# A hybrid decoder step on one core: a list scheduler that accounts for the SBUF port shared by VectorE and GpSimd

## The chip, the cores and the metric

The kernel runs on 1 core of one Trainium2 chip. The metric is device time in microseconds (us), from one launch to its end. Lower is better.

## The reference, cut to what matters

One inference step of a decoder trunk with two layers, on 528 prompt rows (16 learned meta rows and 512 tokens) and 8 sample rows, 536 in all, with 1024 columns each, in float32. Each layer is:

```
x = x + 0.5 * SwiGLU_1(RMSNorm(x))
x = x + W_o(sig(gA) * RWKV7(.) + sig(gB) * ShortConv(.))
x = x + 0.5 * SwiGLU_2(RMSNorm(x))
```

RWKV7 is, for each of 16 heads of 64, a recurrence over rows with a matrix state S:

```
Sa = S a_t
S = S * w_t + Sa b_t^T + v_t k_t^T
y_t = S r_t
```

The prompt starts from S = 0; the 8 sample rows take one step each from a given state. The outputs are y for prompt and sample and all new states.

## The kernel before, in words

**Stages.** A feed-forward stage (`ffn`), the mixer of layer 0 (`mixer`), two feed-forwards, the mixer of layer 1, and a last feed-forward with the final norm. Activations lie with features on 128 partitions and rows along the free dimension. Weights come in tiles of 128 x 1024 (`load_split`): a DMA to `raw`, ScalarE rounds to `hi`, VectorE subtracts (`lo = raw - hi`, two inputs in SBUF), and each product is three passes, hi*hi, hi*lo and lo*hi (`mm3`).

**The mixer.** Heads go in 8 pairs p. `stage_k(p)` projects k and r, computes decays and the Gram products of 11 chunks of 48 rows, and inverts the triangular matrix of each chunk. `stage_v(p)` projects v and prepares `P1`. `chain(p)` runs over the 11 chunks in series: products `cq` on TensorE with steps `rh`, `rd`, `ud`, `sx`, `sd` between them on VectorE and ScalarE; its last state goes out by DMA to `o_swkv`. `gnorm(p)` is the group norm (`wm`), `stage_m(p)` the merge. The loop issues chain(p-1), gnorm(p-1), stage_k(p+1), stage_v(p) in this order. Forty gated projections (`gated_parts`, drawn by `fill`) have low priority and fill in between. `sample` makes the step of the 8 sample rows: eight slices of the state through GpSimd and VectorE operations of 512 columns (names s, t, VB, sm), then DMAs through `yd` to `yb`, transposes and products `ws`. After it the merged rows `mh` go into the product with `w_o` (acc<-mh).

**The inverse** (in `stage_k`, lines 1025 to 1071). The Gram blocks `GT` go by DMA to DRAM (`td`) and back as `Ta`, so that each of 88 partitions holds one half-chunk with half of its columns. Then 46 GpSimd operations, 23 products `pr` and 23 sums into `Xinv`, one after another. The result goes by DMA to `xd` and back as the diagonal blocks of `Yd`. For two groups of chunks, 6 and 5 (`SPL`), the function `step` then issues three rounds on TensorE into PSUM tile `w`, each evicted by ScalarE: transposes of Yd into `x1` (name w1; in the profile MATMUL w<-cst,Yd, as it is a product with the identity), `off` times x1 into `x2` (w2), and x2 times Yd back into Yd (w3). The chain's product cq<-rd,Yd needs the result. Tile w shares a PSUM bank with `cq` and `wm` of the pairs of the same parity.

**What sets the order.** Nothing is issued in program order. Class `Sched` records every operation (all show as line 271, in `issue`, the line that emits them), with its dependencies and a price (`price`, lines 140 to 164), and `flush` (lines 284 to 336) simulates the five engines' queues: it takes the engine that can go on earliest, and on it, of the operations that are ready at that time, the one with the smallest sequence number less `boost`. This fixes each engine's instruction order. On the chip each engine then takes its instructions in that order and waits where an input is late. `offer` (lines 246 to 263) hands an operation to its queue once its buffers are free. All DMAs are on the queue of SyncE (SP). The prices that the change touches, in us for n columns:

```
VectorE       0.07 + n/960, two inputs in SBUF outside the feed-forward n/860; three inputs 0.13
GpSimd        0.2 + n*3e-3, in the feed-forward 0.1 + n*3.1e-3
```

`nc.ffn` is the flag that tells which; `ffn` sets and clears it.

Of the kernel before, what the change touches and what calls it, by code (L numbers as in the profile page):

```python
# [12 lines left out]
PSUM = bass.MemoryType.PSUM  # L13
DRAM = bass.MemoryType.DRAM
# [30 lines left out]
            vector=('bv', 'ka', 'kh', 'kql', 'kt', 'm', 'mb', 'rk', 'rnip', 'rt', 's1', 's3a', 'sl', 'u', 'yl', 'zg')),  # L45
       dict(boost={'k': 1500, 'v': -1000, 'c': 2000, 'g': 100, 'f': -3000, 'm': -50, 's': 1000, 'i': 1500, 'w': 50, 'e': -2000, 'h': -2000},
            ka=4, gated=[0, 3, 0, 0, 1, 0, 0, 1, 1, 0, 2, 2, 1, 0, 0, 1, 0, 0, 1, 4, 1, 0, 1, 0, 1, 1, 0, 1, 1, 1, 0, 0],
            same=0, inv=(),
            vector=('bv', 'kh', 'kql', 'kt', 'm', 'mb', 'rk', 'rt', 's3a', 'sl', 'u', 'yl', 'zg'))]
FIRST = -300  # L50
NORM = 1000
SETUP = -60
# [21 lines left out]

class Op:
    __slots__ = ("seq", "eng", "fn", "args", "kw", "cost", "lat", "npred", "succ", "ready", "prio", "tiles", "first",
                 "tab", "cols0", "cols")


class Slots:  # L80
# [17 lines left out]
class Sched:  # L98
# [13 lines left out]
    def __init__(self, tc):  # L112
        self.nc = tc.nc
        for e in ENGINES:
            setattr(self, e, Engine(self, e))
        self.ops, self.acc, self.free, self.slots, self.life = [], {}, {}, {}, {}
        self.same, self.ffn = 0, False
        self.tick, self.cols, self.fast = 0, 0.0, False
        self.table, self.end, self.gate, self.dma, self.boost, self.kept, self.coming = None, 0.0, 0.0, 0.0, 0, [], []

# [19 lines left out]
    def price(self, eng, fn, out, ins, kw):  # L140
        n = self.width(out)
        if fn == "dma_start":
            return 0.48, 4 * n * out.shape[0] / self.DMA_RATE
        if eng == "tensor":
            if fn == "transpose" or kw.get("is_transpose"):
                return n / 1200 + 2e-3, self.HOP
            return (max(n, 256) / 2400 + 12e-3 if ins[0].dtype == F32R else n / 600 + 6e-3), self.HOP
        if eng == "vector":
            if fn == "memset":
                return 8e-3 + n / 960, self.HOP  # L150
            if fn == "reciprocal":
                return 0.12 + n * 6.16e-3, self.HOP
            if fn == "tensor_reduce":
                n = self.width(ins[0])
            fixed = 0.13 if len(ins) > 2 else 0.07
            if not self.ffn and len(ins) > 1 and all(x.tensor.space != PSUM for x in ins):
                return fixed + n / 860, self.HOP
            return fixed + n / 960, self.HOP
        if eng == "scalar":
            psum = any(x.tensor.space == PSUM for x in ins + [out])  # L160
            return (0.05 if psum else 0.095) + (0.09 if "scale" in kw else 0) + n / 1200, self.HOP
        if self.ffn:
            return 0.1 + n * 3.1e-3, self.HOP
        return 0.2 + n * 3e-3, self.HOP

    def add(self, eng, fn, args, kw):
        o = Op()
        o.seq, o.eng, o.fn, o.args, o.kw = len(self.ops), eng, fn, args, kw
        out = kw["out"] if "out" in kw else args[0]
        ins = [x for x in list(args) + list(kw.values()) if hasattr(x, "tensor") and x is not out]  # L170
        o.cost, o.lat = self.price(eng, fn, out, ins, kw)
        o.tab = TABLES.get(kw.get("func")) if eng == "scalar" else None
        o.succ, o.ready, o.prio, o.first, o.tiles, o.npred = [], 0.0, o.seq - self.boost, [], [], 0
        if eng == "tensor":
            o.cols0 = (o.cost - 12e-3) * 2400
            o.cols = o.cols0 * ins[0].shape[0] / 128
        w = (kw["lhsT"] if "lhsT" in kw else args[1]) if eng == "tensor" else None
        preds, needs, opens = {}, {}, {}
        for ap, wr in [(x, False) for x in ins] + [(out, True)]:
            t = ap.tensor  # L180
            if not hasattr(t, "tag_meta"):
                continue
            n = t.name
            if n not in self.acc:
                self.acc[n] = [], []
                if t.space != DRAM:
                    key = str(t.cap_key)
                    if key not in self.slots:
                        self.slots[key] = Slots(key.rsplit('_', 2)[1], t.bufs or t.tag_meta.bufs, self.gate)
                    self.life[n] = Life(self.slots[key], o)  # L190
                    self.slots[key].line.append(n)
                    o.first.append(n)
            if n not in o.tiles:
                o.tiles.append(n)
                if n in self.life:
                    lf = self.life[n]
                    lf.left += 1
                    opens[id(lf.opener)] = lf.opener
                    if n in lf.slots.held:
                        lf.slots.held[n] = None  # L200
            b = self.box(ap)
            writes, reads = self.acc[n]
            for c, q in writes + reads if wr else writes:
                if c[0] < b[1] and b[0] < c[1] and c[2] < b[3] and b[2] < c[3]:
                    preds[id(q)] = q
                    if not wr:
                        needs[id(q)] = 3 if ap is w and w.dtype == F32 else 2
            if wr:
                for a in (writes, reads):
                    a[:] = [x for x in a if not (b[0] <= x[0][0] and x[0][1] <= b[1] and b[2] <= x[0][2] and x[0][3] <= b[3])]  # L210
                writes.append((b, o))
            else:
                reads.append((b, o))

        for q in {**opens, **preds}.values():
            if q is o:
                continue
            kind = needs.get(id(q), 1 if id(q) in preds else 0)
            if q.succ is None:
                self.follow(q, o, kind)  # L220
            else:
                q.succ.append((o, kind))
                o.npred += 1
        self.ops.append(o)
# [21 lines left out]
    def offer(self, o):  # L246
        for n in o.first:
            s = self.life[n].slots
            if s.line[0] != n or len(s.held) >= s.bufs and all(x is None for x in s.held.values()):
                s.waiting.append(o)  # L250
                return
        first, o.first = o.first, []
        for n in first:
            s = self.life[n].slots
            s.line.pop(0)
            o.ready = max(o.ready, s.gate)
            if len(s.held) >= s.bufs:
                old = min((x for x in s.held if s.held[x] is not None), key=s.held.get)
                o.ready = max(o.ready, s.held.pop(old))
            s.held[n] = None  # L260
        heapq.heappush(self.wait[o.eng], (o.ready, o.seq, o))
        for n in first:
            self.retry(self.life[n].slots)
# [22 lines left out]
    def flush(self):  # L286
# [8 lines left out]
        for _ in range(len(self.ops)):  # L295
            t, e = min((max(self.free.get(e, 0.0), 0.0 if avail[e] else self.wait[e][0][0]), e)
                       for e in ENGINES if avail[e] or self.wait[e])
            while self.wait[e] and self.wait[e][0][0] <= t:
                o = heapq.heappop(self.wait[e])[2]
                heapq.heappush(avail[e], (o.prio, o.seq, o))  # L300
            o = heapq.heappop(avail[e])[2]
# [12 lines left out]
                self.load_table(o.tab)  # L314
            if e == "tensor":
                c = self.clocked(o, t)
            self.free[e] = o.ready = t + c
            if o.fn == "dma_start":
                self.dma = max(self.dma, o.ready + self.DMA_FIXED / 2) + o.lat
# [34 lines left out]
class Build:  # L354
# [246 lines left out]
    def ffn(self, sp, X, w1, w2, l, gname, **kw):  # L601
# [38 lines left out]
            A.activation(out=t, in_=t, func=AF.Silu)  # L640
            self.sg = t

        nc.ffn = True
        ag = [plain(f, 0, False) for f in range(2)]
        rest()
        q = [gate_out(a, f) for f, a in enumerate(ag)]
# [123 lines left out]
                gi += 1  # L770
        while late:
            late.pop()()
        nc.ffn = False
        d = sp.tile([P, 1], F32, tag="d", name="d", bufs=1)
        nc.scalar.activation(out=d, in_=self.sg[:, :1], func=AF.Sqrt, scale=0.0)
        for g in fills + ffout(gi):
# [3 lines left out]
    def mixer(self, l, xh, xl, mD):  # L780
# [8 lines left out]
        with ExitStack() as ctx:  # L789
# [144 lines left out]
            def stage_k(p):  # L934
# [122 lines left out]
                for c0, c1 in SPL:  # L1057
                    n = c1 - c0
                    x1, x2 = (pp.tile([P, 6 * C], F32, tag="tH", name=t, bufs=3)[:C, :n * C].rearrange("p (c q) -> p c q", c=n)
                              for t in ("x1", "x2"))  # L1060

                    def step(fn, out, name):
                        w = psp.tile([P, 512], F32, tag=f"c{p % 2}", name=name, bufs=1)
                        for i in range(n):
                            fn(w[:C, i * C:(i + 1) * C], c0 + i)
                        A.activation(out=out, in_=w[:C, :n * C].rearrange("p (c q) -> p c q", c=n), func=AF.Copy)

                    step(lambda o, c: T.transpose(o, Yd[:C, c, :C], cst["id"][:C, :C]), x1, "w1")
                    step(lambda o, c: T.matmul(out=o, lhsT=off[:C, c, :], rhs=x1[:, c - c0, :], start=True, stop=True), x2, "w2")
                    step(lambda o, c: T.matmul(out=o, lhsT=x2[:, c - c0, :], rhs=Yd[:C, c, C:], start=True, stop=True),  # L1070
                         Yd[:C, c0:c1, C:], "w3")
# [541 lines left out]
```

## Time and profile before

| | us |
|---|---|
| median of 3 runs | 2998.84 (2996.69 to 3001.02) |
| the profiled execution, its own time | 2998.38 |
| its span, first to last instruction | 2996.6 |
| TensorE busy | 2873.9 (96%) |
| VectorE busy | 2134.4 (71%) |
| ScalarE busy | 1360.5 (45%) |
| GpSimd busy | 572.8 (19%) |

The profile is of one execution. Busy times are shares of the span. PE is TensorE, PEld its weight loads, DVE VectorE, ACT ScalarE, POOL GpSimd, SPq the queue of SyncE that issues DMAs. By the stretches of the profile, mixer 0 lies from about 405 to 1118 us, the two feed-forwards to 1885, mixer 1 to 2600, and the last feed-forward behind it. PEclk is the granted clock of TensorE, 1.00 at its higher level (2.4 GHz) and 0.50 at its lower (1.2 GHz). In a row of a view, the part in brackets or behind the bar is the time that the engine sat idle before the instruction, and what ended it.

### The profile page before, as it was taken

To read this page: it belongs to the slowest core of one execution; us is meant where nothing else is said; L and a number is where in the kernel's file an instruction comes from. 1 tells how busy PE (TensorE), PEld (TensorE's weight loads), DVE (VectorE), ACT (ScalarE), POOL (GpSimd) and SP (SyncE) were. 2 spreads that over 40 slices of the span, in tenths; PEclk is the share of its full clock that TensorE was granted. 3 is DMA by queue.
4 is the path that set the end of the run, shared out by engine and by line. 5 is a ranking of instruction groups with operands and counts; after the bars stand their busy time and mean duration, and the time that the engine had idled before them with its cause. 6 is when DMAs were issued, how large, how long until landed. Compare 5 with 4: busy or idle time off the path is not lost.

```text
span 2996.6 us, 57546 instructions
## 1 busy us (share of the span) xinstructions
PE 2873.9 (96%) x23026; PEld 2807.0 (94%) x23026; DVE 2134.4 (71%) x3995; ACT 1360.5 (45%) x2278; POOL 572.8 (19%) x1120
## 2 busy tenths in 40 slices
PE   8999998999999989999999999999999998799997
PEld 8999998899999889999999999989999998799997
DVE  8767666776766868777686766767776678587774
ACT  5444453454444335444444444534454443454443
POOL 1000024222233620000000001333431527100001
PEclk9999999999999999999999999999999999899998
DMA  3232332223222463233323333332232233623232
GB/s 127 96 106 89 121 92 62 71 74 95 78 73 73 144 203 99 89 103 99 109 72 103 96 96 114 95 81 68 70 87 77 64 113 121 200 89 100 95 108 77
DMA packets 219516, 294.22 MB, mean 98 GB/s; under 512 B 119824, under 2 KB 128784, under 8 KB 219248
## 3 DMA queue, kind: packets, MB, share of 16 engines
q1 hardware_dynamic: 219248, 290.54, 31.7%
q8 instruction: 181, 2.97, 0.4%
q14 instruction: 87, 0.71, 0.1%
HBM read 256.38 MB, written 34.10 MB: 97 GB/s over the span
## 4 chain that ended last, share of the span: by engine, by line
PE 63%; DVE 8%; DMA 5%; ACT 2%; POOL 2%; issue 2%; SPq 1%; DVEq 0%; ACTq 0%; POOLq 0%
PE acc L271 20%; PE a L271 12%; PE x L271 9%; PE cq L271 4%; PE y L271 4%; DVE lo L271 2%; PE wg L271 2%; PE au L271 2%; PE ag L271 2%; PE z L271 2%; DMA raw<-in_f_in 2%; PE w L271 2%; PE wp L271 1%; ACT hi L271 1%; POOL pr L271 1%
## 5 line engine op out<-in xcount | busy, mean ns | idle before, releaser
L271 ACT ACTIVATE hi<-raw 128x1024 fp32r<-128x1024 f32 (+4 forms) x460 | 388.0, 845 | 484.6 <-PE acc L271 181.2
L271 DVE TENSOR_TENSOR lo<-raw,hi 128x1024 fp32r<-128x1024 f32 (+4 forms) x460 | 451.7, 983 | 54.3 <-ACT hi L271 47.7
L271 PE MATMUL acc<-xh,lo 128*128 128x268 f32 (+1 forms) x2112 | 480.8, 300 | 8.9 <-DVE lo L271 8.8
L271 PE MATMUL acc<-xh,hi 128*128 128x268 f32 (+1 forms) x2112 | 478.9, 300 | 9.4 <-ACT hi L271 3.7
L271 PE MATMUL acc<-xl,hi 128*128 128x268 f32 (+1 forms) x2112 | 481.4, 299 | 0.0
L271 PEld LDWEIGHTS acc<-xh,hi 128*128 128x128 f32 x2112 | 341.7, 191 | 16.3 <-ACT hi L271 6.9
L271 PEld LDWEIGHTS acc<-xh,lo 128*128 128x128 f32 x2112 | 342.8, 191 | 13.7 <-DVE lo L271 12.3
L271 PEld LDWEIGHTS acc<-xl,hi 128*128 128x128 f32 x2112 | 343.5, 191 | 1.0
L271 PE MATMUL a<-hh,lo 128*128 128x268 f32 (+1 forms) x1408 | 287.3, 285 | 0.0
L271 PE MATMUL a<-hl,hi 128*128 128x268 f32 (+1 forms) x1408 | 287.3, 285 | 0.0
L271 PE MATMUL a<-hh,hi 128*128 128x268 f32 (+1 forms) x1408 | 287.1, 285 | 0.0
L271 POOL MEMSET wide<- 128x104 f32 (+1 forms) x7 | 1.3, 188 | 1338.4 <-DVE lo L271 1261.8
L271 PE MATMUL x<-xh,hi 128*128 128x268 f32 (+1 forms) x864 | 246.6, 286 | 0.8 <-ACT sn L271 0.8
L271 PE MATMUL x<-xl,hi 128*128 128x268 f32 (+1 forms) x864 | 246.7, 286 | 0.0
L271 PE MATMUL x<-xh,lo 128*128 128x268 f32 (+1 forms) x864 | 246.3, 285 | 0.0
L271 ACT ACTIVATE hi<-s 128x1024 fp32r<-128x1024 f32 x144 | 152.0, 1057 | 171.0 <-DVE s L271 121.5
L271 PEld LDWEIGHTS a<-hh,lo 128*128 128x128 f32 x1408 | 219.4, 188 | 0.0
L271 PEld LDWEIGHTS a<-hh,hi 128*128 128x128 f32 x1408 | 218.8, 188 | 0.0
L271 PEld LDWEIGHTS a<-hl,hi 128*128 128x128 f32 x1408 | 218.6, 188 | 0.0
L271 DVE TENSOR_TENSOR lo<-s,hi 128x1024 fp32r<-128x1024 f32 x144 | 173.3, 1220 | 17.1 <-ACT hi L271 16.6
L271 POOL TENSOR_TENSOR pr<-Ta,Xinv 88x22 f32<-88x22 f32 (+16 forms) x368 | 135.8, 369 | 161.5 <-DMA Ta<-td 136.3
L271 DVE SCALAR_TENSOR_TENSOR X<-a,X 128x536 f32<-128x536 f32 (+1 forms) x160 | 113.1, 707 | 74.5 <-PE a L271 74.4
(570 smaller groups left out, 7190.5 us busy)
## 6 DMA issues: line engine op xcount, KB each, us to landing
raw<-in_f_in SPq DMA_DIRECT2D x176, 512.0 KB
raw<-in_w_in SPq DMA_DIRECT2D x132, 512.0 KB
raw<-in_f_out SPq DMA_DIRECT2D x128, 256.0 KB
raw<-in_f_out SPq DMA_DIRECT2D x32, 384.0 KB
raw<-in_w_o SPq DMA_DIRECT2D x32, 256.0 KB
XD<-X SPq DMA_DIRECT2D x16, 268.0 KB
s<-in_swkv SPq DMA_DIRECT2D x16, 256.0 KB
out_o_sswkv<-s SPq DMA_DIRECT2D x16, 256.0 KB
```

Of the source, the lines that this page charges most:

```text
L271: return getattr(getattr(self.nc, o.eng), o.fn)(*o.args, **o.kw)
```

## The change

The planner gets a variable `port`: the time until which the SBUF port of VectorE and GpSimd is taken. An operation counts as a user (`o.port`) if it is GpSimd's, or VectorE's with more than one input of more than one column that lies in SBUF. When one is issued, its start is moved to `port` if that is later, and `port` becomes its start plus 0.7 of its price (SHARE). Both engines' prices become the same inside and outside the feed-forward, and the flag `ffn` goes. The transposes of the inverse (name w1) carry a `pad` of 4.0 us (LATE), which `offer` adds to the time from which each may be taken. The kernel's operations and the tables of priorities `MIX` stay as they are; only the order of the instructions on the five queues can differ.

```diff
+LATE = 4.0
+SHARE = 0.7
...
-            fixed = 0.13 if len(ins) > 2 else 0.07
-            if not self.ffn and len(ins) > 1 and all(x.tensor.space != PSUM for x in ins):
-                return fixed + n / 860, self.HOP
-            return fixed + n / 960, self.HOP
+            return (0.15 if len(ins) > 2 else 0.09) + n / 960, self.HOP
...
-        if self.ffn:
-            return 0.1 + n * 3.1e-3, self.HOP
-        return 0.2 + n * 3e-3, self.HOP
+        return (0.28 + n * 1.7e-3 if fn == "tensor_tensor" else 0.2 + n * 1e-3), self.HOP
...
+        o.pad = self.pad
+        o.port = eng == "gpsimd" or eng == "vector" and sum(
+            x.tensor.space not in (PSUM, DRAM) and self.width(x) > 1 for x in ins) > 1
...
+        o.ready += o.pad
         heapq.heappush(self.wait[o.eng], (o.ready, o.seq, o))
...
+            if o.port:
+                t = max(t, self.port)
+                self.port = t + SHARE * c
             self.free[e] = o.ready = t + c
...
-        nc.ffn = True
...
-        nc.ffn = False
...
+                    nc.pad = LATE
                     step(lambda o, c: T.transpose(o, Yd[:C, c, :C], cst["id"][:C, :C]), x1, "w1")
+                    nc.pad = 0.0
```

## Rows read from the trace of the kernel before

**Rows 1.** The page: busy time of each engine, share of the span, instructions.

```profile
PE 2873.9 (96%) x23026; PEld 2807.0 (94%) x23026; DVE 2134.4 (71%) x3995; ACT 1360.5 (45%) x2278; POOL 572.8 (19%) x1120
```

**Rows 2.** Busy time by stretches: us, then PE, PEld, DVE, ACT, POOL busy, PEclk, DMA.

```profile
405.00:1118.00 713.00, 668.30 (x5289) 638.23 (x5288) 502.55 (x1144) 308.40 (x577) 238.16 (x514) 0.98 0.33 94
1118.00:1885.00 767.00, 765.18 (x6169) 763.64 (x6170) 557.67 (x844) 363.11 (x549) 28.55 (x23) 1.00 0.32 100
1885.00:2600.00 715.00, 669.72 (x5355) 640.10 (x5353) 501.29 (x1142) 314.46 (x584) 261.29 (x538) 0.98 0.33 95
```

**Rows 3.** TensorE's waits: totals (us, times, longest), then four stalls on the timeline.

```profile
PE w L271 <- DMA Yd<-xd: 12.1, 9, 2.9
PE w L271 <- POOL Xinv L271: 4.8, 1, 4.8
...
477.88 0.24 PE L271 MATMUL w<-cst,Yd 48*48 48x48 f32 x1 [4.84 <-POOL Xinv L271]
513.31 0.20 PE L271 MATMUL w<-cst,Yd 48*48 48x48 f32 x1 [2.92 <-DMA Yd<-xd]
885.85 0.20 PE L271 MATMUL w<-cst,Yd 48*48 48x48 f32 x1 [2.24 <-DMA Yd<-xd]
1962.31 0.20 PE L271 MATMUL w<-cst,Yd 48*48 48x48 f32 x1 [2.00 <-DMA Yd<-xd]
```

**Rows 4.** Stretches at the low clock; columns as in rows 2.

```profile
477.70:481.10 3.40, 3.22 (x14) 3.12 (x15) 1.21 (x2) 0.00 (x0) 2.62 (x11) 0.50 0.68 147
573.20:583.40 10.20, 7.67 (x28) 6.21 (x29) 9.43 (x22) 3.08 (x8) 1.40 (x3) 0.50 0.28 91
887.30:890.70 3.40, 3.40 (x19) 3.02 (x18) 2.25 (x4) 0.40 (x1) 0.00 (x0) 0.50 0.78 245
```

**Rows 5.** GpSimd's timeline: first and last operation of the first inverse.

```profile
442.13 0.22 POOL L271 TENSOR_TENSOR pr<-Ta,Xinv 88x23 f32<-88x23 f32 x1 [1.81 <-DMA Ta<-td]
...
467.94 0.22 POOL L271 TENSOR_TENSOR Xinv<-Xinv,pr 88x12 f32<-88x12 f32 x1
```

**Rows 6.** Timeline: two GpSimd operations, and VectorE's that began between them.

```profile
445.00 0.25 POOL L271 TENSOR_TENSOR pr<-Ta,Xinv 88x40 f32<-88x40 f32 x1
445.33 1.19 POOL L271 TENSOR_TENSOR Xinv<-Xinv,pr 88x40 f32<-88x40 f32 x1
...
445.17 1.23 DVE L271 TENSOR_TENSOR lo<-raw,hi 128x1024 fp32r<-128x1024 f32 x1 [1.46 <-ACT hi L271]
```

**Rows 7.** Timeline: Yd written and used; last states of chains one, five and eight of mixer 0.

```profile
485.90 0.40 ACT L271 ACTIVATE Yd<-w 48x288 f32<-48x288 f32 x1 [1.40 <-PE w L271]
...
493.25 0.38 PE L271 MATMUL cq<-rd,Yd 96*96 96x128 f32 x2
...
563.72 0.37 SPq L271 DMA_DIRECT2D out_o_swkv<-sd  x1
...
809.33 0.36 ACT L271 ACTIVATE Yd<-w 48x240 f32<-48x240 f32 x1 [0.93 <-PE w L271]
...
838.83 0.34 SPq L271 DMA_DIRECT2D out_o_swkv<-sd  x1
...
1070.07 0.34 SPq L271 DMA_DIRECT2D out_o_swkv<-sd  x1
```

**Rows 8.** The DMA queue's waits.

```profile
SPq L271 <- POOL Xinv L271: 57.3, 11, 10.1
```

**Rows 9.** End of mixer 1: GpSimd's least held form, its wait, TensorE's stall.

```profile
L271 POOL TENSOR_TENSOR t<-VB,sm 128x512 f32<-128x512 f32 x8 | 8.6, 1070 | 3.2 <-DVE sm L271 1.9 <-PE cq L271 1.3
...
POOL t L271 <- DVE s L271: 18.2, 7, 4.9
...
2558.40 1.02 PE L271 MATMUL ws<-cst,yb 8*128 8x8 f32 x8 [7.65 <-DMA yb<-yd]
```

**Rows 10.** VectorE's groups in mixer 0: busy us, mean ns, idle before.

```profile
L271 DVE TENSOR_TENSOR lo<-raw,hi 128x1024 fp32r<-128x1024 f32 x63 | 81.2, 1288 | 4.0 <-ACT hi L271 2.7 <-PE acc L271 0.5
...
L271 DVE TENSOR_TENSOR sx<-cq,P 128x128 f32<-128x128 f32 x88 | 25.2, 286 | 47.8 <-PE cq L271 47.3
```

More of the change, by code (lines that the diff above doesn't have):

```diff
@@ L76 @@
     __slots__ = ("seq", "eng", "fn", "args", "kw", "cost", "lat", "npred", "succ", "ready", "prio", "tiles", "first",
-                 "tab", "cols0", "cols")
+                 "tab", "cols0", "cols", "pad", "port")
 class Slots:
@@ L116, in __init__ @@
         self.ops, self.acc, self.free, self.slots, self.life = [], {}, {}, {}, {}
-        self.same, self.ffn = 0, False
+        self.same, self.pad, self.port = 0, 0.0, 0.0
         self.tick, self.cols, self.fast = 0, 0.0, False
```

## The prediction

> **What bounds the kernel now.** I first read the page's busy times [rows 1]: TensorE is busy 96% of the span, VectorE 71%, GpSimd 19%. Only idle or slowed TensorE time can be won. The view by stretches shows where that is [rows 2]: in the feed-forward stretch between the mixers TensorE is busy 765.18 of 767.00 us, so nothing is to be had there. In the two mixers it is busy 668.30 of 713.00 and 669.72 of 715.00 us: 44.7 and 45.3 us, together 90.0 us of idle.
>
> Who ended those idle times is in the view of waits [rows 3]. The first step of the inverse, the transposes w<-Yd, waited 12.1 us in 9 places for the DMA that brings Yd, and 4.8 us once where the view names GpSimd's inverse (in truth the same DMA behind it): 16.9 us, the largest single cause. TensorE takes its instructions in order, so it stood although other products were ready. The two longest stalls, 4.84 us until 477.88 and 2.92 us until 513.31, both lie in the first 110 us of mixer 0.
>
> Then the clock, by the stretches behind stalls [rows 4]: right after the stall that ends at 477.88 the granted clock was 0.50, the lower of its two levels, for 3.4 us, and so it was behind that of 885.85; two more such pairs lie in mixer 1 (1962.50 behind the stall that ends at 1962.31, and 2351.60), four in all. Half speed for 3.4 us loses 1.7 us. The long stretch 573.20 to 583.40 has 0.50 too, with 7.67 us busy of 10.20: TensorE had too little work there, mostly steps of the chain. I call this a drought. At full clock its work takes 7.67 / 2 = 3.8 us, so one drought costs 6.4 us.
>
> **Why the transposes come early: the planner's price.** The inverse of a head pair is 46 GpSimd operations over 1,222 column products for each of its two kinds: at the old price 46 x 0.2 + 2444 x 0.003 = 16.5 us. On the chip the first one ran from 442.13 to 468.16, 26.0 us [rows 5]. The reason is visible [rows 6]: a GpSimd operation of 40 columns took 0.25 us, and the next of the same size 1.19 us, because VectorE's subtraction of two SBUF tensors (1.23 us) had begun 0.16 us earlier. GpSimd was held for 1.19 - 0.25 = 0.94 us, until 1.10 us after VectorE's start, 0.89 of its duration.
>
> **The change part by part.** It adds no arithmetic and removes none; all five queues get a new order.
>
> *The port account.* The planner now lets a GpSimd operation, or a VectorE one with two SBUF inputs, begin only when 0.7 of the previous holder's price is over. For the row above it gives 0.7 x (0.09 + 1024/960) = 0.81 us where the trace shows 1.10. The new price of an inverse without the port is 46 x 0.28 + 2444 x 0.0017 = 17.0 us; of the 9.0 us that the first one took beyond, the account covers at most 0.81/1.10, some 6.6 us, and misses 2.4. The Trainium skill (SBUF — State Buffer, Who interferes with whom) says that the first to issue holds the shared pair for the whole instruction and the other fully blocks. By that the wait in the row would have lasted to 1.23 us, where the trace shows 1.10, and the account would miss 0.42 us of it rather than 0.29; what this would do stands as a rival below.
>
> *LATE.* Each of the two groups of transposes in each of 16 inverses becomes eligible 4.0 us later. With the 2.4 us missed, and an old error of up to 26.0 - 16.5 = 9.5 us now mostly priced, all stalls of [rows 3] should go: 16.9 us of waits, and 4 x 1.7 = 6.8 us of clock. What is late next is the use of Yd. Mostly it is covered: in mixer 0 the sixth inverse is written at 809.33 and the chain before it ends only at 838.83, 29 us of cover [rows 7]. The tightest place is the first inverse: its first part is written from 485.90, the chain's product with Yd starts at 493.25. That is 7.3 us, more than 4.0, so I cost it at nothing; without that cover it would be 4 us per mixer. DMAs: on SyncE's queue the writes xd and Yd move back relative to the weight loads. SyncE waited 57.3 us for the inverse in 11 places [rows 8], with weight loads queued behind; moving those loads ahead is a gain or nothing, and I count nothing. The evictions on ScalarE and the chain's shared PSUM bank move with the transposes by the same 4.0 us, under the same cover.
>
> *But not all reaches the end.* In the first 110 us of mixer 0, other products pulled into the two long stalls will be missing in the drought at 573.20. I count these two (4.84 + 2.92 + one clock drop of 1.7 = 9.5 us) as zero between bounds of 0 and 9.5, because the drought is the nearest row. There remain 16.9 - 7.8 = 9.1 us of waits and 3 x 1.7 = 5.1 us of clock: **14.2 us**.
>
> *Cheaper GpSimd in the sample stage.* Its operations of 512 columns were priced 0.2 + 512 x 0.003 = 1.74 us and are now 0.28 + 512 x 0.0017 = 1.15 us before the port; the trace shows 1.07 for the least held form [rows 9]. GpSimd waited 18.2 us in the last 120 us of mixer 1 for VectorE's addition s, because VectorE's queue had been ordered for a slower GpSimd. This path ends late: TensorE stood 7.65 us until 2558.40 for yb, the sample stage's result on its way back through DRAM. Bounds: 0, and the whole 7.65 us. The group norm of the last pair runs just before, and if the sample stage no longer ends last it is late next, so I take half, **3.8 us**.
>
> *VectorE's prices.* Small PSUM operations: 128 columns go from 0.203 to 0.223, where the trace has 0.286: nearer. Two SBUF inputs of 1024 columns go from 1.261 to 1.157, where it has 1.288: further off, which the port is to make up [rows 10]. GpSimd's sums of the norms get cheaper likewise. The rest of the reorder has either sign. Beyond the terms above, 90.0 - 16.9 - 7.65 = 65 us of mixer idle is spread over many small waits; a better order may take a sixth of it, 10 us, a worse one add as much. The rows on either side of the true price (nearer for small operations, further for large) lean neither way, so the value taken is zero. In the feed-forward, the same prices cost nothing: VectorE there is busy 557.67 of 767.00 us and hides behind TensorE.
>
> **Sum.** The profiled execution took 2998.38 us around a span of 2996.6, 0.46 below the median of three, 2998.84. 2998.4 - 14.2 - 3.8 = **2980.4**, say 2980. Against the median that is -0.6%.
>
> **Rivals.**
> *Everything comes through.* If the first stalls count too (9.5) and the tail gives its whole 7.65, the sum is 2998.4 - 16.9 - 6.8 - 7.65 = 2967; with the sixth of the small waits 2957. For it: TensorE works in order, so a stall removed is time back at once. Against: the drought. Chance 0.12.
>
> *The account is too short.* The account misses as much of the hold as the 0.7 leaves out, and an inverse held longest meets its transposes early all the same. If the stalls of 2.24 and 2.00 us with their clock drops stay, 4.2 + 3.4 = 7.6 us of the 14.2 go, and the time is 2988. The rule of the Trainium skill named above (SBUF — State Buffer, Who interferes with whom) is what would bring this about; the 0.89 of the row is milder than it. Chance 0.10; still faster.
>
> *No change: the chain sets the pace.* The eight chains of mixer 0 end between 563.72 and 1070.07 [rows 7], 72.3 us each. If the chain, not TensorE's work, is what the end follows, the removed stalls turn into other idle. For it: the drought, in which little but the chain ran. Against: TensorE is busy 94% of the mixers. Or the new prices leave the order mostly as it was. The time is 2998. Chance 0.16.
>
> *Slower: more droughts.* LATE pulls up to 16 x 2 x 4.0 = 128 us of other products ahead of the transposes. They are the low-priority gated projections, and what is used early is missing while a chain runs alone. Its place is the chains' middle, its price 6.4 us for each drought. Three more cost 19.2 us and cancel the 18.0 won: that is the point where it decides. Five more, one in about three of the 16 chains, give 2998.4 - 18.0 + 32.0 = 3012. For it: one such drought is there already, and the priorities stand as they were for the old prices. Against: it is one in 16 chains so far. Chance 0.22.
>
> **How the numbers follow.** About 0.2%, 6 us, is what a measurement of this kernel can tell from no change, so 2992.8 to 3004.8 is "same". My forecast, 2980 (its own range 2970 to 2990), has 0.40; with the first two rivals faster has 0.62, same 0.16, slower 0.22. The range must leave out at most 2 in 10: down to 2957, the lower bound, and up to 3010, which leaves out a good half of the slower case and little else.
>
> **What would show it.** Right: the transposes' waits on Yd fall from 16.9 us to under 3; the clock drops behind them vanish; GpSimd's wait for s in the tail falls below 10 us and the wait for yb below 4; mixer idle falls from 90 to about 70 us; the feed-forward stretch stays within 1 us. Wrong: new stretches at the low clock with chain products only; waits on Yd moved from the transposes to the chain's first product; or the transposes' stalls gone with the mixers as long as before.

## The result and the profile after

The change makes the kernel faster by 43 us where 18 were forecast: 2956.86 us (median of 4, 2954.42 to 2959.83) against 2999.93 (median of 4), ratio 0.9857, 95% interval 0.9840 to 0.9874. It lies just under the range's lower end of 2957.

The page after, busy time of each engine [rows 1]:

```profile
span 2955.4 us, 57453 instructions
## 1 busy us (share of the span) xinstructions
PE 2873.6 (97%) x23026; PEld 2811.0 (95%) x23026; DVE 2135.9 (72%) x3995; ACT 1362.6 (46%) x2284; POOL 587.7 (20%) x1120
```

TensorE is busy for the same time as before, 2873.9 then and 2873.6 now. The span lost 41.2 us, and 40.9 of it is idle time of TensorE. Where, is in the stretches. I cut both runs at the same events: from the first projection of a mixer to the last product with W_o behind it. Here the kernel before; columns are the stretch, its length, and busy time of PE, PEld, DVE, ACT, POOL, then PEclk, the DMA engines' busy share and GB/s.

```profile
387.10:1139.30 752.20, 706.02 (x5577) 675.37 (x5576) 530.92 (x1192) 329.78 (x609) 250.04 (x530) 0.98 0.34 98
1139.30:1873.30 734.00, 733.66 (x5933) 732.71 (x5932) 534.49 (x805) 346.43 (x523) 19.80 (x15) 1.00 0.31 97
1873.30:2618.90 745.60, 698.25 (x5578) 667.67 (x5577) 520.08 (x1176) 327.80 (x605) 269.66 (x546) 0.98 0.34 98
2618.90:2996.60 377.70, 361.38 (x2980) 359.41 (x2978) 269.62 (x409) 174.58 (x268) 13.27 (x10) 0.98 0.29 93
```

And the kernel after:

```profile
390.10:1115.40 725.30, 701.89 (x5577) 674.54 (x5577) 530.96 (x1193) 325.85 (x607) 260.47 (x530) 0.98 0.35 102
1115.40:1848.90 733.50, 733.09 (x5933) 732.40 (x5933) 536.35 (x804) 346.28 (x524) 19.81 (x15) 1.00 0.30 97
1848.90:2580.10 731.20, 702.11 (x5578) 671.54 (x5577) 520.71 (x1176) 334.14 (x614) 274.22 (x546) 0.98 0.34 100
2580.10:2955.40 375.30, 360.19 (x2980) 358.57 (x2979) 267.75 (x409) 173.94 (x267) 12.84 (x10) 0.98 0.30 95
```

Mixer 0 is 26.9 us shorter and mixer 1 14.4; the two feed-forwards between them lost 0.5 us, the last stretch 2.4, and the start gained 3.0 on the other side. Idle time in the mixers went from 46.2 to 23.4 and from 47.4 to 29.1 us, 41.0 together. TensorE's busy time in them moved by about 4 us each, down in mixer 0 and up in mixer 1.

TensorE's waits after, whole run [rows 3, 9]: us in total, times, longest.

```profile
PE cq L273 <- DVE rd L273: 5.5, 6, 2.6
PE acc L273 <- DVE lo L273: 5.4, 10, 1.9
PE a L273 <- DVE X L273: 4.8, 4, 2.4
...
PE wg L273 <- DVE mv L273: 3.4, 1, 3.4
...
PE ws L273 <- DMA yb<-yd: 0.4, 1, 0.4
```

There is no row for the transposes any more: 16.9 us are gone. The wait for yb fell from 7.65 to 0.4. Together that is 24 of the 41 us of idle; the other 17 are many small waits. Towards the end of mixer 1, GpSimd's own wait for VectorE's s [rows 9] fell from 18.2 to 4.1 us, and the product with yb came almost without a stall; first the view of GpSimd's waits, over 100 us in each kernel:

```profile
POOL t L273 <- DVE s L273: 4.1, 5, 1.2
```

and the timeline of TensorE, where the number in brackets is the wait ahead of the instruction:

```profile
2513.26 0.41 PE L273 MATMUL ws<-cst,yb 8*128 8x8 f32 x4 [0.41 <-DMA yb<-yd]
```

**The stall on yb stood in a longer hole.** Here is the tail of mixer 1, from the end of its last gated projection to the last product with W_o, before and after (columns as above), and then the part of the one before that ran at the low clock:

```profile
2542.60:2618.90 76.30, 54.22 (x402) 51.70 (x403) 41.11 (x69) 31.31 (x61) 9.14 (x9) 0.84 0.62 203
2523.10:2580.10 57.00, 51.16 (x393) 49.30 (x393) 35.10 (x58) 28.49 (x55) 8.51 (x7) 0.97 0.67 219
...
2546.10:2570.00 23.90, 8.62 (x37) 7.59 (x38) 13.27 (x27) 10.46 (x28) 2.04 (x3) 0.50 0.65 204
```

Before, TensorE was idle 22.1 us of the tail: steps of the last group norm, the wait for yb, the sample's products and the wait for the merged rows followed one another, with no projection left to put in between. The first product with W_o came 22.3 us behind the last projection. After, it comes 0.8 us behind, idle is 5.8 us, and the tail is 19.3 us shorter for nearly the same number of products (402 and 393). The rest of mixer 1 got 4.9 us longer.

**LATE moves more than 4 us.** The timeline after, where Yd of the first inverse is written and used [rows 7]:

```profile
498.74 0.41 ACT L273 ACTIVATE Yd<-w 48x288 f32<-48x288 f32 x1 [1.44 <-PE w L273]
...
515.59 0.36 ACT L273 ACTIVATE Yd<-w 48x240 f32<-48x240 f32 x1 [1.27 <-PE w L273]
...
517.17 0.39 PE L273 MATMUL cq<-rd,Yd 96*96 96x128 f32 x2
```

Before, the two parts were written 4.6 us apart (485.90 and 490.45); now it is 16.9 us. In `offer` each transpose of a group gets the 4.0 us, and those behind the first become eligible only when the first has opened the PSUM tile: 8 us for a group, 16 for both in the plan. On the chip it can be far more. The sixth inverse of mixer 0 [rows 7] was written at 809.33, long before its chain (timeline of before):

```profile
855.42 0.38 PE L271 MATMUL cq<-rd,Yd 96*96 96x128 f32 x2
```

After (timeline), it is written 54 us later and used at once, although GpSimd ended this inverse 24.5 us earlier than before (767.69 against 792.22):

```profile
863.10 0.37 ACT L273 ACTIVATE Yd<-w 48x240 f32<-48x240 f32 x1 [1.05 <-PE w L273]
...
864.70 0.38 PE L273 MATMUL cq<-rd,Yd 96*96 96x128 f32 x2
```

Of the 16 chains, two began within 2.5 us of the end of their Yd's last write before, and five after. The first chain starts 24 us later (493.25 before) and the last of mixer 0 ends 5 us later, yet the mixer ends 24 us earlier. Other work moved. Before (timeline), the last projection ended behind the last chain (1070.07) and the first product with W_o followed it:

```profile
1077.67 0.40 PE L271 MATMUL acc<-lgh,lo 128*128 128x268 f32 x2
1083.34 0.82 PE L271 MATMUL acc<-mh,hi 128*128 128x268 f32 x2 [2.94 <-ACT mh L271]
```

After, the projections are done and W_o begins 20 us ahead of the last chain's end, and runs between the chain's steps:

```profile
1054.95 0.41 PE L273 MATMUL acc<-lgh,lo 128*128 128x268 f32 x2
1055.29 0.49 PE L273 MATMUL acc<-mh,hi 128*128 128x268 f32 x2
...
1075.33 0.38 SPq L273 DMA_DIRECT2D out_o_swkv<-sd  x1
```

### The profile page after: what moved, and what is told of

The parts are those of the page before. It is cut to its first block, busy times and chain, and to the rows that moved or that the text cites. A ratio compares the mean times of both kernels' runs of the same rounds, so it can differ in the third digit from the quotient of the medians.

```text
span 2955.4 us, 57453 instructions
## 1 busy us (share of the span) xinstructions
PE 2873.6 (97%) x23026; PEld 2811.0 (95%) x23026; DVE 2135.9 (72%) x3995; ACT 1362.6 (46%) x2284; POOL 587.7 (20%) x1120
## 4 chain that ended last, share of the span: by engine, by line
PE 86%; DVE 6%; ACT 2%; DMA 2%; issue 2%; POOL 1%; SPq 0%; DVEq 0%; ACTq 0%; POOLq 0%
PE acc L273 26%; PE a L273 17%; PE x L273 13%; PE y L273 7%; PE cq L273 5%; PE wg L273 3%; PE au L273 3%; PE z L273 3%; PE ag L273 3%; PE w L273 2%; DVE lo L273 2%; PE wp L273 2%; DMA raw<-in_f_in 1%; ACT hi L273 1%; POOL t L273 1%
## 5 line engine op out<-in xcount | busy, mean ns | idle before, releaser
L273 POOL TENSOR_TENSOR pr<-Ta,Xinv 88x22 f32<-88x22 f32 (+16 forms) x368 | 149.6, 407 | 146.9 <-DMA Ta<-td 122.2
```

The source lines that it names most:

```text
L273: return getattr(getattr(self.nc, o.eng), o.fn)(*o.args, **o.kw)
```

## The experiments

Theory A: the stalls at the transposes come back whole as time, and LATE carries that. Theory B: the truer prices do it. Theory C: any new order of the mixers is a draw, and 43 us is a lucky one. D to H came later. Ratios are against the kernel before, run beside each. Idle is TensorE's in the two mixers, as the sum of its waits longer than 0.15 us (1 to 3 us less than all idle time); Yd is what the products into w waited for Yd, yb the wait for yb; all in us, from one profiled execution each, which can lie off the median (3005.15 against 2994.91 us in e5).

| run | ratio [95%] | idle | Yd | yb |
|---|---|---|---|---|
| before | 1 | 92 | 17.2 | 7.7 |
| after | 0.9857 [0.9840, 0.9874] | 51 | 0.0 | 0.4 |
| e1 LATE only | 0.9931 [0.9910, 0.9951] | 78 | 2.2 | 15.7 |
| e2 prices only | 0.9954 [0.9937, 0.9972] | 81 | 8.7 | 1.2 |
| e3 no LATE | 0.9953 [0.9935, 0.9971] | 76 | 3.0 | 1.1 |
| e4 no port | 0.9911 [0.9882, 0.9940] | 68 | 0.4 | 0.5 |
| e5 before, HOP 0.21 | 0.9978 [0.9967, 0.9989] | 88 | 15.6 | 13.8 |
| e6 after, HOP 0.21 | 0.9920 [0.9903, 0.9936] | 68 | 0.0 | 0.8 |
| e7 LATE 8 | 1.0185 [1.0166, 1.0204] | 105 | 0.0 | 1.6 |
| e8 SHARE 1 | 1.0007 [0.9995, 1.0020] | 73 | 0.0 | 0.9 |
| e9 before, HOP 0.19 | 1.0092 [1.0060, 1.0123] | 106 | 21.3 | 13.6 |
| e10 before, HOP 0.22 | 1.0006 [0.9982, 1.0031] | 87 | 13.7 | 13.3 |
| e11 after, HOP 0.19 | 0.9872 [0.9843, 0.9901] | 55 | 0.0 | 1.7 |
| e12 after, HOP 0.22 | 0.9835 [0.9798, 0.9871] | 52 | 0.0 | 0.7 |
| e13 LATE only, HOP 0.22 | 0.9944 [0.9921, 0.9966] | 75 | 2.0 | 11.2 |
| e14 no LATE, HOP 0.22 | 0.9940 [0.9912, 0.9967] | 71 | 1.6 | 0.9 |
| e15 SHARE 1, HOP 0.22 | 0.9988 [0.9968, 1.0007] | 74 | 0.0 | 0.6 |
| e16 LATE 8, HOP 0.22 | 1.0198 [1.0167, 1.0229] | 100 | 0.0 | 0.9 |
| e17 4 us once | 0.9895 [0.9870, 0.9921] | 63 | 0.0 | 0.8 |
| e18 16 us once | 0.9861 [0.9837, 0.9884] | 64 | 0.0 | 0.0 |

**The parts alone (e1 to e4).** The edits are against before (e1) and against after (e2 to e4):

```diff
# e1
+        o.ready += o.pad
+                    nc.pad = LATE
                     step(lambda o, c: T.transpose(o, Yd[:C, c, :C], cst["id"][:C, :C]), x1, "w1")
+                    nc.pad = 0.0
# e2
-LATE = 4.0
-SHARE = 0.7
+LATE = 0.0
+SHARE = 0.0
# e3
-LATE = 4.0
+LATE = 0.0
# e4
-SHARE = 0.7
+SHARE = 0.0
```

> The kernel before with LATE = 4.0 for the transposes alone: old prices, no port account. Theory A (the stalls at the transposes come through whole, and LATE is what removes them): their waits on Yd fall from 16.9 us to about 5, as the old price of an inverse is still up to 9.5 us short, and the time falls by 12 to 17 us with the clock drops, to about 2985; the rest of the 43 us is the port account's. Theory B (the truer prices of VectorE and GpSimd carry the gain all over the mixers): under 8 us, above 2990. Theory C (the gain is a draw: any new order of the mixers shifts the time by 10 to 20 us either way): anywhere from 2980 to 3015, with waits on Yd gone all the same.

> The new prices alone (SHARE = 0, LATE = 0). Theory A: the transposes still wait 12 to 20 us, as the inverse is priced 17.0 us against 16.5 before, and the time stays within 8 us of 2999. Theory B: VectorE's and GpSimd's cheaper prices without the port make VectorE wait for GpSimd; slower than before by 5 to 20 us, as only price and port together are true. Theory C: anywhere from 2980 to 3015.

> The change without LATE (new prices and port account, LATE = 0). Theory A: waits on Yd of 5 to 10 us remain, and the time is 2970 to 2980. Theory B: 2957 to 2963, as the port account alone moves the transposes by what the inverse really takes. Theory C: not between the two, or slower than before.

> The change without the port account (new prices and LATE = 4.0, SHARE = 0). Theory A: waits on Yd of about 5 us remain, time 2975 to 2985. Theory B: most of the gain is gone, 2985 to 3000. Theory C: unrelated to e1 and e2: LATE is not worth the same here as it is in e1.

Measured: 2981.56, 2989.61, 2987.83 and 2976.97 us. No part carries the gain: LATE alone is worth 0.7%, prices and port without LATE 0.5%, all together 1.4%; prices alone give 0.5% as well, prices with LATE 0.9%. Theory A's time came near for e1 and came for e4, but not for e2 (8.7 us of waits, not 12 to 20) or e3: there the transposes wait only 3.0 us and 2987.83 is still some 30 us behind the whole change. Theory B falls with e2, e3 and e4; its forecast that prices alone are slower was wrong. With LATE alone, TensorE's waits (view of waits of e1) on Yd are down, and the wait for yb is there:

```profile
PE ws L274 <- DMA yb<-yd: 15.7, 2, 12.8
PE w L274 <- DMA Yd<-xd: 2.2, 2, 1.6
```

The timeline of e1 shows where the longest one stands:

```profile
2542.10 1.02 PE L274 MATMUL ws<-cst,yb 8*128 8x8 f32 x8 [12.80 <-DMA yb<-yd]
```

It is longer than the 7.7 us of before, but that is not LATE's doing: the redrawn kernels before, without LATE, have 13.3 to 13.8 us (table). Mixer 0 of e1 was 21 us shorter than before, mixer 1 3.9 us longer. In e3 (waits of TensorE) both waits are small:

```profile
PE w L273 <- DMA Yd<-xd: 3.0, 4, 1.8
PE ws L273 <- DMA yb<-yd: 1.1, 2, 0.8
```

The wait for yb is nearly gone in every run with the new prices (1.7 us at most), the waits on Yd in every run with LATE (2.2 at most). But the new prices and the port account bring the waits on Yd down without LATE too, and it pays less than they were: in mixer 0 of e3 the transposes wait 0.4 us in all, and the chain's products cq 17.2 us (0.3 and 17.5 in e14), where cq waited 11.1 before (5.1 and 5.8 in e5 and e10) and 9.5 after. Part of the wait had moved.

**Draws of the order (e5, e6, e9 to e12) and larger settings (e7, e8).**

```diff
# e5, e6; 0.19 in e9, e11; 0.22 in e10, e12
-    HOP = 0.2
+    HOP = 0.21
# e7
-LATE = 4.0
+LATE = 8.0
# e8
-SHARE = 0.7
+SHARE = 1.0
```

> The kernel before, with the planner's default delay between engines (HOP) at 0.21 instead of 0.20 us: no price becomes truer by it, but the order is drawn anew. Theory C (a draw): the time differs from before by 8 us or more either way, up to the size of what single parts gave (9 to 22 us). Theory D (the parts' gains are systematic: LATE and the port each leave TensorE more independent products between dependent steps): within 6 us of before, and the waits on Yd are again 12 to 20 us.

> The kernel after, with HOP at 0.21 instead of 0.20 us: the same redraw of the order. Theory C: the 2957 was a lucky draw, and this one is 2970 to 2990. Theory D: 2951 to 2963, waits on Yd below 1 us.

> The kernel after with LATE = 8.0. Waits on Yd are gone at 4.0 already. Theory D: within 8 us of 2957, as the cover of 7 us at the first inverse of a mixer is just used up and elsewhere there is 29 us. Theory C: 2965 to 2990. The rival of more droughts (other products used up early): above 2970, with new long stretches at the low clock in the middle of the mixers.

> The kernel after with SHARE = 1.0: the port is held for the whole price of an operation, nearer to the 0.89 of the row of before (1.10 us against a price of 1.157, so 0.95 of the price). Theory D: 2950 to 2962, as the account gets a little truer. Theory C: 2965 to 2990.

Measured: 2994.91, 2978.49, 3058.28 and 3007.20 us. One hundredth of a microsecond in HOP took 19 us off the gain (0.9857 against 0.9920): theory D's number for e6 failed and theory C seemed near. In e5 the waits on Yd are back (15.6 us), and the time lies 7 to 9 us under before, between the two theories. e7 and e8 are slower than theories C and D had them; for e7 only the rival of more droughts allows its time. So I redrew both kernels twice more.

> The kernel before with HOP = 0.19: another draw of the order. Theory E (the change has a systematic part, the removed waits on Yd and on yb with their clock drops, of about 18 to 25 us; the rest of its 43 us and of the losses of e7 and e8 is the draw): 2985 to 3015, waits on Yd of 10 to 20 us again. Theory C (draw alone): the same range, but no lower or higher on average than the redrawn kernels after.

> The kernel before with HOP = 0.22. As e9: Theory E 2985 to 3015 with waits on Yd of 10 to 20 us; theory C the same range.

> The kernel after with HOP = 0.19. Theory E: 2960 to 2990, faster than its pair e9, waits on Yd and yb below 2 us. Theory C: 2985 to 3010 although these waits are gone.

> The kernel after with HOP = 0.22. Theory E: 2960 to 2990, faster than its pair e10, waits on Yd and yb below 2 us. Theory C: 2985 to 3010 although these waits are gone.

Measured: 3028.02, 3000.17, 2962.06 and 2950.85 us. Pair by pair (HOP 0.19, 0.20, 0.21, 0.22), the ratios of after to before are 0.978, 0.986, 0.994 and 0.983: mean 0.985. The change is faster in all four, by 16 to 66 us, and the slowest kernel after is 16 us faster than the fastest before: theory C falls, and 43 us is no lucky draw but close to the mean of the four, 44. Theory E held in sign and place, not in size (18 to 25 us; e9 is also 13 us above its range and e12 9 us below). A single draw of before scatters over 33 us, one of after over 28. The waits come and go with the change, not with the draw (waits of TensorE in e9):

```profile
PE w L271 <- DMA Yd<-xd: 15.6, 8, 3.7
PE ws L271 <- DMA yb<-yd: 13.6, 2, 12.3
PE w L271 <- POOL Xinv L271: 5.7, 1, 5.7
```

and in e12:

```profile
PE ws L273 <- DMA yb<-yd: 0.7, 2, 0.5
```

Mean of the four draws, from the table: idle 93 to 56.5 us, of it Yd 17.0 to 0, yb 12.1 to 0.9, all other waits 64 to 56. The mean granted clock of the profiled executions rose from 0.982 to 0.987 besides (HOP 0.20, 0.21, 0.19, 0.22: 0.985, 0.979, 0.981, 0.981; then 0.987, 0.985, 0.986, 0.989), and TensorE's busy time fell by 6 us in the mean.

**Parts and settings in the best draw (e13 to e16).** The kernels of e1, e3, e8 and e7 with HOP = 0.22.

> LATE alone (old prices, no port account) in the draw HOP = 0.22, where before took 3000.2 and after 2950.9. Theory F (LATE carries the waits on Yd and their clock drops, the new prices the wait for yb, and each is there alone): waits on Yd below 3 us, the wait for yb still 8 to 13 us, time 2970 to 2985. Theory G (LATE and the account only work together): within 8 us of 3000.

> The change without LATE in the draw HOP = 0.22. Theory F: waits on Yd of 2 to 8 us, no wait for yb, time 2975 to 2990. Theory G: within 8 us of 3000.

> SHARE = 1.0 in the draw HOP = 0.22. If e8 lost by its draw: 2950 to 2980. If the loss is a mechanism (the planner holds VectorE back from the port longer than the chip does, and the chain's steps on VectorE are ordered behind): 2990 to 3015, with longer low-clock stretches in the mixers, 60 us or more in mixer 0.

> LATE = 8.0 in the draw HOP = 0.22. If e7 lost by its draw: 2950 to 2985. If by the rival of more droughts (other products used up early, the last chain of a mixer runs alone): above 3020, with low-clock stretches of over 20 us at the ends of both mixers.

Measured: 2984.09, 2985.37, 2998.37 and 3060.39 us. Theory F's times came in both parts: 17 and 18 us by the ratios, each alone; together 50. By the same ratios the parts of the first draw give 21 and 14, together 43. So the whole is 8 and 15 us more than the sum, which is less than the scatter of one draw: theory G is not needed, and whether the parts help each other stays open. F's reason is half right, since the waits on Yd are nearly gone without LATE (1.6 us in e14).

Where each part acts can be read from the lengths of the mixers in all runs. The tail of mixer 1, cut as in the result, took 73.6 to 77.5 us in the six kernels with the old prices (before in four draws, e1, e13) and 54.6 to 59.3 in the twelve with the new prices and no LATE of 8; prices alone (e2) have 58.6. So the new prices close that hole. Mixer 0 took 742 to 770 us in the seven kernels without LATE, and 720 to 735 in six of the seven with LATE = 4.0 on every transpose and no SHARE of 1.0; e6, with 748.1, is the exception, and the slowest draw of after. With SHARE = 1.0 it took 764 and 754.

The losses of e7 and e8 repeat, so they have causes. That of LATE = 8 is the rival of droughts as e16 foretold it, at the ends of the mixers: the longest low-clock stretches there are 37.6 and 30.7 us in e7, 47.8 and 27.3 in e16. Two stretches of e7, the whole of mixer 0 and 67 us near its end (columns as above):

```profile
388.10:1182.10 794.00, 731.78 (x5576) 686.89 (x5575) 529.73 (x1191) 327.67 (x607) 261.10 (x530) 0.95 0.32 92
1078.00:1145.00 67.00, 50.42 (x287) 41.80 (x287) 45.33 (x111) 19.74 (x52) 20.43 (x17) 0.72 0.47 155
```

and the timeline of e7 where its last chain hands over the state:

```profile
1144.68 0.34 SPq L273 DMA_DIRECT2D out_o_swkv<-sd  x1
```

The last projection ended at 1078, where it did before, but the last chain at 1144.7, 75 us later. For those 67 us TensorE was busy 50.42, at a mean clock of 0.72. The two parts of Yd of the first inverse now lie 28.5 us apart, and thirteen of the 16 chains of e7 begin within 2.5 us of the last part of their Yd (five at LATE = 4.0): the chain has become the pace. For SHARE = 1.0 the idle time is down like in other runs (73 against 92 us), but the granted clock is 0.978 in e8, 0.981 in e15, and in e8 TensorE was busy 31 us longer than before for the same products (page of e8):

```profile
PE 2904.9 (97%) x23026; PEld 2829.8 (94%) x23026; DVE 2140.2 (71%) x3995; ACT 1366.3 (45%) x2285; POOL 586.6 (19%) x1120
```

e15's time is the one foretold for a mechanism, but its sign is not there: mixer 0 has 51 us at the low clock, not 60. Why those orders have so much of the low clock was not settled.

**What of LATE counts (e17, e18).** Only the first transpose of an inverse is delayed, by 4.0 and by 16.0 us:

```diff
+                    def flip(o, c):
+                        nc.pad = LATE if c == 0 else 0.0
+                        T.transpose(o, Yd[:C, c, :C], cst["id"][:C, :C])
+                        nc.pad = 0.0
-                    nc.pad = LATE
-                    step(lambda o, c: T.transpose(o, Yd[:C, c, :C], cst["id"][:C, :C]), x1, "w1")
-                    nc.pad = 0.0
+                    step(flip, x1, "w1")
```

> The change with the delay of 4.0 us on the first transpose of each inverse alone, so that it does not add up. Theory A (the removed waits are LATE's worth): waits on Yd below 1 us and 2952 to 2965, as with the whole LATE. Theory H (the whole shift of 17 us is its worth: gated projections are done before the last chain ends): waits on Yd below 1 us all the same, the last gated projection of mixer 0 at 1065 to 1078 as without LATE, and 2975 to 2990.

> The change with 16.0 us once on the first transpose of each inverse, the same whole shift as LATE = 4.0 but not spread over the groups. Theory H: the last gated projection of mixer 0 at 1050 to 1060, and 2950 to 2970. Theory A: within 10 us of e17. Theory C (each of these orders is a draw): no relation to the place of the last gated projection.

Measured: 2974.12 and 2963.24 us. Both are without waits on Yd. Against e3 (0.9953), 4 us once are worth 0.6%, the whole shift 0.9 to 1.0%, at once (0.9861) or spread (0.9857). The last projections of mixer 0 end at 1076.6 in e3, 1068.1 in e17, 1061.9 in e18 and 1054.4 after: in theory H's order, though e18 missed its 1060 and e17 came in just under H's range. But that place does not order the other runs: the last projection ends at 1042.4 in e1 (2981.56 us) and at 1061.3 in e5, a kernel before (2994.91). Nor does theory A hold: e3 had only 3.0 us of waits on Yd left to remove, and e17 is 17 us faster by the ratios. Both steps, e3 to e17 and e17 to e18 (11 us), are smaller than the scatter of draws. So what of LATE counts remains open; shown is that the whole of it, on top of prices and port, is worth 1.0% in both draws (e3 to after, e14 to e12).

## Why the prediction was wrong, point by point

- **Where the idle is, and that transposes and yb are the two causes:** right for the 24 of 92 us that they name. Both are all but gone, in all four draws. The feed-forward stayed within 0.5 us. By its terms the forecast was 6.0 us for mixer 0 (waits 4.3, clock 1.7) and 12.1 for mixer 1 (waits 4.9, clock 3.4, tail 3.8); measured are 26.9 and 14.4, so the miss is in mixer 0.
- **"But not all reaches the end"** failed; with the rest of the order, below, it is where the error lies. I had counted the stalls of the first 110 us of mixer 0 as zero, since other products pulled in there would be missing in the drought at 573.20. The first 200 us of mixer 0, before and after, show that the drought did not grow but all but went:

```profile
387.10:587.10 200.00, 181.72 (x1403) 172.96 (x1402) 133.20 (x294) 90.08 (x149) 68.73 (x179) 0.96 0.29 77
390.10:590.10 200.00, 193.80 (x1549) 187.34 (x1549) 140.38 (x298) 93.46 (x148) 76.49 (x180) 0.99 0.31 84
```

TensorE's idle time there fell from 18.3 to 6.2 us. One reading is that no products were missing because, in the kernel before, projections were left over behind the last chain (until 1077.67), so there was work to pull forward. No run isolates that, and in e5 and e10 (kernels before) no projections are left over behind the last chain of mixer 0, though the change gains 16 and 49 us there too. One drought, 13.7 us at the low clock from 1031.2, did appear beside the last chain after:

```profile
1031.20:1044.90 13.70, 11.27 (x49) 10.01 (x50) 9.04 (x19) 1.56 (x6) 1.72 (x1) 0.50 0.57 191
```

- **The tail, half of 7.65:** mis-sized, and its upper bound too. The whole wait went (0.4 left), over the draws 11.2 us of 12.1, and the tail around it got 19.3 us shorter. The 23.9 us at the low clock from 2546.10, the longest such stretch of the kernel before, stand in no row that I read. GpSimd's wait for s fell from 18.2 to 4.1 us, as forecast.
- **The clock, 5.1 us:** in this draw the busy time of TensorE did not change (2873.9 to 2873.6), so the term gave nothing net; the four drops behind the stalls went and others came. In the mean of the four draws busy time fell by 6 us, near the term.
- **The rest of the order, value zero:** 17 us of idle in this draw, 9 in the mean of four. I had bounded it by 10. This and the zeroed stalls (7.8 us of waits) make up nearly all of the 25 us that the forecast was short.
- **LATE as 4.0 us and a cover of 7.3:** wrong in the code and in the row. The delays add up to 16 us in the plan and to 54 us at the row of the sixth inverse, whose 29 us of cover were used up, and the first chain waits for the second part of Yd (490.45, 2.8 us before its use), as the planner opens the chain's PSUM bank only behind the last tile w. That it cost nothing was luck of the forecast: the first chain began 24 us later, but at 4.0 the chain was not yet the pace. At 8.0 it is, so the rival "the chain sets the pace" had the mechanism of e7 and e16, not of this change.
- **The rivals:** "everything comes through" (2957) has the measured time, but partly by luck: its clock term of 6.8 us gave nothing in this draw, its tail was too small, the small waits gave 17 and not 10, and another draw took 2978. Its reason, that a stall removed is time back at once, fails in e3, e8, e14 and e15. "The account is too short" did not happen: no wait on Yd is left, though the first inverse took 29.1 us on the chip, and even without LATE only 3.0 us are (e3). The Trainium skill's rule beside it (SBUF — State Buffer, Who interferes with whom), a hold for the whole instruction, is what SHARE = 1.0 plans by, and here that plan loses the gain (e8, e15). The traces agree with the rule all the same, and my 0.89 of the row was a misreading (see the last section): the hold lasts to VectorE's end. "More droughts" is right as a mechanism for 8 us, where the loss begins somewhere above 4; its place was the mixers' ends, not the chains' middle.

## What to carry to other kernels

A named stall on an engine that takes its instructions in order is a candidate for time back, not yet time back. e3, e8, e14 and e15 lost 21 to 24 of the 25 us of named stalls and gained between nothing and 18 us: other waits and the granted clock took the rest. Nor is the stall's own length an upper bound: where no other work is left, as in the tail of mixer 1, look at the whole hole around it (7.65 us of stall, 22.1 us of idle). Discount a stall only on a row that shows the engine short of work; here the drought that I used for this nearly vanished itself. A change of a planner's prices must be judged over several draws of the order: one draw moved the time by up to 27 us for no reason of its own, and a difference between two parts that is smaller than this shows nothing.

## What the runs showed of the hardware

**How long GpSimd is held.** In the row of before [rows 6] the held GpSimd operation ended at 446.52, 0.12 us after VectorE's (446.40). The timeline after has the same form again, begun 0.05 us behind VectorE's instead of 0.16:

```profile
843.65 1.28 POOL L273 TENSOR_TENSOR pr<-Ta,Xinv 88x40 f32<-88x40 f32 x1
...
843.60 1.23 DVE L273 TENSOR_TENSOR lo<-raw,hi 128x1024 fp32r<-128x1024 f32 x1
```

It ended 0.11 us after VectorE's. So it is in all 47 cases of the two traces in which an operation of the inverse began during such a subtraction and took over 0.25 us more than when free: it ended 0.07 to 0.20 us after VectorE's, the later the more columns it has (0.07 to 0.08 with 12 columns, 0.11 to 0.12 with 40, 0.17 to 0.19 with 72), and it made no difference when it began (0.01 to 0.44 us after VectorE's start). The hold lasted as long as VectorE's instruction; of the 0.25 us that 40 columns take when free, only about half came behind it. I had put all of it there, and so read 0.89.

**What a truer plan does.** Inverses were not shorter for being planned with the hold: 26.0 us before and 29.1 after for the first, 23.1 and 24.7 in the mean of the eight of mixer 0, and 30.5 with SHARE = 1.0 (e8). The plan does not take the hold away; it only puts other work where the wait is.

**The clock where work runs out.** In the tail of mixer 1 before, TensorE had 8.62 us of work in 23.9 us, and the granted clock was 0.50 (1.2 GHz) all that time.
